# Converting the weights to bf16 once, in device memory, and giving the weight loads and the small transfers different DMA queues

## The chip, the cores and the metric

The kernel runs on all 8 cores of one Trainium2 chip. Every core does the same work on its own part of the batch. The metric is device time in microseconds (us) of the slowest core, and lower is better. Cores 0 to 3 are one die of the chip, cores 4 to 7 the other.

Names in the profiles: PE is TensorE (matmuls) and PEld its weight loads, DVE is VectorE, ACT ScalarE, POOL GpSimd and SP SyncE. HBM is the device memory, SBUF the memory on the core, and a DMA moves data between or within them. The granted clock is the share of its full clock at which PE was allowed to run.

- An execution on 8 cores can fall into a slower state, in which one die or both run matmuls at a lower granted clock: in one execution of e1 a core of die 0 took 40042 us at 0.719 and a core of die 1 40826 us at 0.701.
- The experiments ran on two chips that are called the second and the third here; the first comparison is taken as another, the first chip (the record names no chip for it). In the experiments the clock was often lower: the kernel before took 38.8 ms in the first comparison (clock 0.703 to 0.705 in the profiled run) and in fast executions 39.5 to 39.7 ms there (0.674 to 0.695). Whole times of different chips are therefore never compared. Inside a trace, the short stages that the argument needs are compared, and most of those are bound by DMA (share 0.93 to 1.08 in the conversions and the sample FFNs before) or by waits, not by the clock.
- Ratios compare fast runs with fast runs. The medians quoted with the experiments are of all runs, slow ones too, so a ratio is not quite that of the medians.

## The reference, cut to what matters

It is a four-layer encoder. The FFN weights are 1024 x 4096 and 4096 x 1024, and all weights arrive as float32.

```python
def encoder_layer(x, prm, ...):
    x = x + 0.5 * swiglu_ffn(rms_norm(x, ffn1_norm), ffn1_w_gate, ffn1_w_up, ffn1_w_down)
    proj = rms_norm(x, mix_norm) @ w_in
    # S5 state space, differential attention, conv module, gMLP: the "mixer"
    x = x + concat(a_out, b_out, c_out, d_out) @ w_out
    x = x + memory_cross_attention(rms_norm(x, xattn_norm), mem_k, mem_v, xattn_wq, xattn_wo)
    x = x + 0.5 * swiglu_ffn(rms_norm(x, ffn2_norm), ffn2_w_gate, ffn2_w_up, ffn2_w_down)
# ... the small inputs, the outputs and the second request group are cut
```

A core handles 4096 prompt tokens and 256 sample tokens. Both use the same weights.

## The kernel before

The kernel has its own small scheduler. It keeps one instruction list for each engine, and derives each wait from the last writer and the readers of a buffer. The tokens are taken in nine tiles: eight prompt tiles of 512 tokens and one sample tile of 256. Each tile goes through all four layers, so every weight is loaded nine times.

Weights go through a ring of four SBUF slots of 1 MB (128 x 4096 bf16). The loads are issued on GpSimd's queue (`pool`). They read float32 from HBM and write bf16 into SBUF, so the DMA itself converts: the page below has 2270.65 MB on that queue, where bytes are counted as written, and 4716.93 MB read from HBM in all.

```python
NRING = 4
def w_issue_upto(n):                       # ...
        tag, src, shp = wq_list[i]         # src: a float32 view of the weight in HBM
        slot = ring[i % NRING]
        # ...
        P.DMA("pool", dst, src)

def w_next(tag):
    i = wstate["taken"]
    w_issue_upto(i + NRING - 1)            # at step i, the loads up to i+2 are issued
    # ...
```

One FFN takes 24 ring slots and 768 matmuls of 512 columns:

```python
def ffn(l, which, N, gidx):
    A.reset()                              # a barrier, see below
    rmsnorm_to_h(N, gains_sb[:, l, gidx, :])
    # ...
    for half in range(2):
        for jc in range(4):
            wg = w_next(which + "g")
            wu = w_next(which + "u")
            # 4 x (8 + 8) matmuls, one silu and one product each
        for oc in range(4):
            wd = w_next(which + "d")
            # 2 x 16 matmuls, one residual add each
```

Every stage (FFN, mixer, cross-attention) opens with `A.reset()`, which puts a barrier into all five instruction lists. A barrier waits for all engines and for every DMA that had been issued by then in program order:

```python
def barrier(self, with_dma=True):
    for e in COMPUTE + ("sp",):
        # ... e waits for the instruction counts of the other engines, and
        for key, cnt in self.dma_cnt.items():
            if self.waited[e].get(key, 0) < 16 * cnt:
                waits[key] = 16 * cnt
```

The main loop is `prep()` (tables, and the keys and values of the memory), then for each tile and each layer `ffn("ffn1")`, `mixer`, `xattn`, `ffn("ffn2")`. Small inputs, outputs and saved keys and values go over SyncE's queue (`sp`), apart from the small ones that are converted on the way, such as `wsT`, which share GpSimd's queue with the ring.

The softmax here doesn't subtract the row's maximum and nothing guards it: scores larger than these inputs give would overflow.

## Time and profile before

The median of the 20 runs is 38774 us (38658 to 38866). The profiled run's slowest core is core 1.

| what | before |
|---|---|
| span of core 1 | 38652.5 us |
| start and preparation | 435 us |
| eight prompt tiles | 3754 us (first) to 4795 us (last) |
| sample tile | 3823 us |
| one FFN, prompt tile / sample tile | about 200 / 172 us |

Stage times in this document run from the first matmul of a stage's normalisation to the first of the next stage's, in one core's trace. The last normalisation of a tile counts to the next tile.

First some lines of the page of the kernel before: busy time of the engines; DMA share in 40 slices; queues as packets, MB and share of 16 engines; the chain of work that ended last; and the ring's loads with count, size and median time from issue to landing.

```profile
span 38652.5 us, 393341 instructions; the slowest of 8 cores (38538.2 to 38652.5 us)
...
PE 22710.2 (59%) x127946; PEld 11272.6 (29%) x127946; DVE 11651.9 (30%) x20752; ACT 7756.2 (20%) x15712; POOL 3130.1 (8%) x3366
...
DMA  3444444444444433434444433344432344325665
...
q0 software_dynamic: 2898592, 2270.65, 42.2%
q1 hardware_dynamic: 92896, 260.74, 1.9%
...
HBM read 4716.93 MB, written 84.78 MB: 124 GB/s over the span
...
PE 48%; DVE 21%; DMA 15%; issue 8%; ACT 5%; POOL 2%; DVEq 1%; ACTq 0%; POOLq 0%; SPq 0%
...
ring<-ffn_w_gate POOLq DMA_DIRECT2D x576, 1024.0 KB, 12.2
ring<-ffn_w_up POOLq DMA_DIRECT2D x576, 1024.0 KB, 15.2
ring<-ffn_w_down POOLq DMA_DIRECT2D x576, 1024.0 KB, 13.0
```

No engine is full. The chain runs through PE for half the time. That DMA is 15% of the chain and busy 42% overall says nothing yet about where a faster load would help. The stretch view does. Its columns are the stretch and its length, busy us of PE, PE weight load, DVE, ACT and POOL, the granted clock, the DMA share (the times of all packets added up, so that a full stretch can come out slightly above 1, as the 1.07 below) and GB/s written. The first line is a prompt FFN, the second two sample FFNs, on core 1.

```profile
10220.00:10408.00 188.00, 171.25 (x768) 75.69 (x768) 33.09 (x48) 25.18 (x41) 22.25 (x23) 0.96 0.92 126
35640.00:35970.00 330.00, 203.79 (x1543) 162.66 (x1540) 46.19 (x105) 32.15 (x76) 44.48 (x46) 0.82 1.07 148
```

In the prompt tile the DMA engines are almost full, but PE is busy 171 of 188 us: the loads just keep up. In the sample tile each matmul has half the columns, the loads are the same size, and DMA is the limit (share 1.07, PE busy 204 of 330 us). The timeline of PE in that prompt FFN shows how small the waits are. Columns: start, length, what, and in brackets the idle time before it and what ended it.

```profile
10220.05 32.20 PE L201 MATMUL PS<-h,ring 128*128 128x512 bf16 x136 [12.44 <-DVE h L245]
10252.66 13.97 PE L201 MATMUL PS<-h,ring 128*128 128x512 bf16 x64 [0.42 <-DMA ring<-ffn_w_up]
10269.50 13.93 PE L201 MATMUL PS<-h,ring 128*128 128x512 bf16 x56 [2.86 <-DMA ring<-ffn_w_up]
```

A last pair of lines is from the waits view of core 1: total us, times, longest. The second is for `wsT`, the gMLP weight that stands behind ring loads in GpSimd's queue.

```profile
PE PS L201 <- DMA ring<-ffn_w_up: 540.4, 243, 8.7
...
DVE arena L222 <- DMA arena<-wsT: 383.2, 36, 13.8
```

### The profile page before, as it was taken

To read this page: it belongs to the slowest core of one execution; us is meant where nothing else is said; L and a number is where in the kernel's file an instruction comes from. 1 tells how busy PE (TensorE), PEld (TensorE's weight loads), DVE (VectorE), ACT (ScalarE), POOL (GpSimd) and SP (SyncE) were. 2 spreads that over 40 slices of the span, in tenths; PEclk is the share of its full clock that TensorE was granted. 3 is DMA by queue.
4 is the path that set the end of the run, shared out by engine and by line. 5 is a ranking of instruction groups with operands and counts; after the bars stand their busy time and mean duration, and the time that the engine had idled before them with its cause. 6 is when DMAs were issued, how large, how long until landed. Compare 5 with 4: busy or idle time off the path is not lost.

```text
span 38652.5 us, 393341 instructions; the slowest of 8 cores (38538.2 to 38652.5 us)
## 1 busy us (share of the span) xinstructions
PE 22710.2 (59%) x127946; PEld 11272.6 (29%) x127946; DVE 11651.9 (30%) x20752; ACT 7756.2 (20%) x15712; POOL 3130.1 (8%) x3366
## 2 busy tenths in 40 slices
PE   3555555556666655556656655666765666764444
PEld 1222222222222222223223322332333323333333
DVE  3333333333333333332332233223223232222222
ACT  0111111111111112122112222221222212221111
POOL 0000000000000000000000000000000000001111
PEclk8777777777777766767777766677766677666666
DMA  3444444444444433434444433344432344325665
GB/s 70 69 69 69 74 69 69 69 74 70 70 70 70 65 57 58 62 56 65 71 71 74 59 49 53 61 72 72 67 50 48 57 72 72 56 43 80 82 81 79
DMA packets 2993473, 2556.56 MB, mean 66 GB/s; under 512 B 187135, under 2 KB 2905983, under 8 KB 2984192
## 3 DMA queue, kind: packets, MB, share of 16 engines
q0 software_dynamic: 2898592, 2270.65, 42.2%
q1 hardware_dynamic: 92896, 260.74, 1.9%
q8 instruction: 1088, 17.83, 0.2%
q14 instruction: 897, 7.35, 0.1%
HBM read 4716.93 MB, written 84.78 MB: 124 GB/s over the span
## 4 chain that ended last, share of the span: by engine, by line
PE 48%; DVE 21%; DMA 15%; issue 8%; ACT 5%; POOL 2%; DVEq 1%; ACTq 0%; POOLq 0%; SPq 0%
PE PS L201 48%; DMA ring<-ffn_w_up 8%; DVE arena L254 5%; DVE arena L222 5%; ACT arena L219 4%; DVE arena L265 4%; DVE h L245 2%; DVE arena L235 2%; POOL arena L222 2%; DMA arena<-wsT 1%; DMA arena<-cv 1%; ACT L219 1%; DMA arena<-Bx 1%; DVEq L165 1%; DVE arena L245 1%
## 5 line engine op out<-in xcount | busy, mean ns | idle before, releaser
L201 PE MATMUL PS<-h,ring 128*128 128x512 bf16 (+1 forms) x41472 | 9018.2, 381 | 2292.1 <-DVE h L245 1677.3
L201 PEld LDWEIGHTS PS<-h,ring 128*128 128x128 bf16 x41472 | 4167.0, 101 | 7179.5 <-issue 3023.9
L201 PE MATMUL PS<-arena 128*128 128x64 bf16 (+4 forms) x12354 | 1282.7, 265 | 6696.2 <-POOL arena L222 4082.5
L219 ACT ACTIVATE arena<-PS 128x512 f32<-128x512 f32 (+7 forms) x4298 | 2247.2, 524 | 11509.8 <-PE PS L201 10354.7
L201 PE MATMUL PS<-arena,ring 128*128 128x512 bf16 (+1 forms) x19712 | 4192.1, 375 | 449.9 <-DVE arena L222 285.9
L219 ACT ACTIVATE arena<-PS,alibi 128x256 bf16<-128x256 f32 (+1 forms) x8960 | 3677.0, 458 | 1548.1 <-PE PS L201 1538.3
L222 DVE TENSOR_TENSOR arena<-arena,PS 128x512 bf16<-128x512 f32 (+2 forms) x2376 | 1564.6, 659 | 7685.0 <-PE PS L201 7022.0
L201 PEld LDWEIGHTS PS<-arena 128*128 128x128 bf16 (+2 forms) x12354 | 782.6, 132 | 7168.5 <-issue 7130.9
L201 PE MATMUL PS<-arena,VAh 128*65 128x128 bf16 x16896 | 2725.0, 312 | 227.1 <-ACT arena L219 227.1
L201 PEld LDWEIGHTS PS<-arena,ring 128*128 128x128 bf16 x19712 | 1944.4, 100 | 2710.4 <-issue 723.8
L201 PE MATMUL PS<-QT,KTh 32*128 32x128 bf16 x16896 | 2347.9, 275 | 547.5 <-ACT arena L219 289.6
L219 ACT ACT_TABLE_LOAD x513 | 658.2, 1283 | 8944.3 <-DVE arena L245 5753.2
L222 DVE TENSOR_TENSOR PS<-PS,diag 128x128 f32<-128x128 f32 (+1 forms) x1152 | 307.6, 289 | 5862.1 <-PE PS L201 5799.4
L201 PEld LDWEIGHTS PS<-arena,VAh 128*65 128x65 bf16 x16896 | 1678.5, 160 | 795.4 <-issue 331.0
L254 DVE RECIPROCAL arena<-PS 64x512 f32<-64x512 f32 (+3 forms) x480 | 1379.0, 2873 | 1371.7 <-PE PS L201 1371.7
L254 DVE RECIPROCAL arena<-arena 128x512 f32<-128x512 f32 (+5 forms) x374 | 1065.3, 2848 | 2408.0 <-ACT arena L219 2324.0
L245 DVE SCALAR_TENSOR_TENSOR x<-PS,x 128x512 f32<-128x512 f32 (+1 forms) x1152 | 762.9, 662 | 3292.1 <-PE PS L201 3292.1
L201 PE MATMUL PS<-arena,ones_b 128*128 128x512 bf16 (+2 forms) x1616 | 700.5, 571 | 1689.9 <-ACT arena L219 1689.9
L265 DVE TENSOR_TENSOR_SCAN arena<-arena,sst 128x64 f32<-128x64 f32 x4096 | 1437.7, 351 | 451.5 <-DVE arena L222 40.2
L201 PEld LDWEIGHTS PS<-QT,KTh 32*128 32x128 bf16 x16896 | 1004.8, 99 | 1884.1 <-issue 1633.9
L219 ACT ACTIVATE arena<-x 128x512 bf16<-128x512 f32 (+1 forms) x1224 | 741.1, 605 | 3966.6 <-issue 2107.5
L222 DVE TENSOR_TENSOR arena<-PS,arena 128x512 f32<-128x512 f32 (+2 forms) x1316 | 803.3, 662 | 2095.8 <-PE PS L201 2074.9
(110 smaller groups left out, 12910.1 us busy)
## 6 DMA issues: line engine op xcount, KB each, us to landing
ring<-ffn_w_gate POOLq DMA_DIRECT2D x576, 1024.0 KB, 12.2
ring<-ffn_w_up POOLq DMA_DIRECT2D x576, 1024.0 KB, 15.2
ring<-ffn_w_down POOLq DMA_DIRECT2D x576, 1024.0 KB, 13.0
ring<-w_in POOLq DMA_DIRECT2D x144, 1024.0 KB, 10.9
arena<-s5tab SPq DMA_DIRECT2D x36, 2560.0 KB, 10.6
ring<-w_out POOLq DMA_DIRECT2D x72, 1024.0 KB, 12.4
arena<-Cx POOLq DMA_DIRECT2D x72, 512.0 KB, 6.2
ring<-xattn_wq POOLq DMA_DIRECT2D x36, 1024.0 KB, 9.3
```

What stands on the lines that cost most here:

```text
L165: e.wait_ge(sems[k], v)
L201: self.S.op("pe", lambda e: e.matmul(o.ap, lhsT=l.ap, rhs=r.ap, start=start, stop=stop, **kw), reads=[l.buf, r.buf], writes=[o.buf])
L219: self.S.op("act", lambda e: e.activation(out=o.ap, in_=i.ap, func=func, **kw), reads=reads, writes=[o.buf])
L222: self.S.op(eng, lambda e: e.tensor_tensor(out=o.ap, in0=a.ap, in1=b.ap, op=op), reads=[a.buf, b.buf], writes=[o.buf])
L235: self.S.op(eng, lambda e: e.tensor_scalar(out=o.ap, in0=a.ap, scalar1=v1, scalar2=None, op0=op0), reads=reads, writes=[o.buf])
L245: self.S.op(eng, lambda e: e.scalar_tensor_tensor(out=o.ap, in0=a.ap, scalar=v, in1=b.ap, op0=op0, op1=op1), reads=reads, writes=[o.buf])
L254: self.S.op("dve", lambda e: e.reciprocal(out=o.ap, in_=i.ap), reads=[i.buf], writes=[o.buf])
L265: self.S.op("dve", lambda e: e.tensor_tensor_scan(out=o.ap, data0=d0.ap, data1=d1.ap, initial=iv, op0=ALU.mult, op1=ALU.add), reads=reads, ...
```

## The change

Intent: read each float32 weight once instead of nine times. A DMA from HBM to HBM converts it into a bf16 copy; the nine ring loads then read half the bytes. A ring load no longer converts and is issued on SyncE's queue, and the small transfers move to GpSimd's. The core of the diff:

```diff
+    def convert_weights(l_, only=None):
+        order = ["ffn1_w_gate", "ffn1_w_up", "ffn1_w_down", "w_in", "w_out", "xattn_wq", "xattn_wo",
+                 "ffn2_w_gate", "ffn2_w_up", "ffn2_w_down"]
...
+                half = rows // 2
+                P.DMA("pool", dst[0:half], src[0:half], grp="cv")
+                P.DMA("pool", dst[half:rows], src[half:rows], grp="cv")
...
-            P.DMA("pool", dst, src)                     # the ring load
+            P.DMA("sp", dst, src)
...
-                wq_list.append((which + "g", kview(g, l, 0, D, c0, 512), (8, 512)))
+                wq_list.append((which + "g", bview(g, l, 0, D, c0, 512), (8, 512)))   # bf16 copy; all weights alike
...
-        P.DMA("sp", dst, src)                           # every small DMA alike
+        P.DMA("pool", dst, src)
...
     def main_program():
+        for l_ in range(L):
+            convert_weights(l_, only=["xattn_wk", "xattn_wv"])
+        convert_weights(0)
         prep()
...
             for l in range(L):
+                if (kind, ti) == tiles[0] and l + 1 < L:
+                    convert_weights(l + 1)
                 ffn(l, "ffn1", N, 0)
```

The two halves of a weight write the same scheduler buffer, so the second half waits until the first has landed. Each core makes its own copies.

Why the queues move along with it: the author left every DMA that converts on GpSimd's queue and gave SyncE the ring loads once they had nothing to convert. In the trace before, all ring loads are issued on GpSimd's queue (576 of each of the three FFN weights); in the trace after, the same numbers on SyncE's, and all of them are bf16 to bf16. No run here tries a cast on another queue.

More of the change, by code (lines that the diff above doesn't have):

```diff
@@ L106, in op, with dma @@
         self._mark(tok, reads, writes)
-    def dma(self, q, fn, reads=(), writes=()):
-        j = self.dma_rr[q]
-        self.dma_rr[q] = (j + 1) % NDMA_SEMS
-        key = "dma_%s_%d" % (q, j)
+    def dma(self, q, fn, reads=(), writes=(), grp=None, ngrp=6):
+        if grp is None:
+            j = self.dma_rr[q]
+            self.dma_rr[q] = (j + 1) % NDMA_SEMS
+            key = "dma_%s_%d" % (q, j)
+        else:
+            j = self.dma_rr.get(grp, 0)
+            self.dma_rr[grp] = (j + 1) % ngrp
+            key = "dma_%s_%d" % (grp, j)
         prev = self.dma_cnt.get(key, 0)
@@ L266, in SCAN, with DMA @@
                   reads=reads, writes=[o.buf])
-    def DMA(self, q, o, i):
+    def DMA(self, q, o, i, grp=None):
         if len(o.ap.shape) > 3 and len(i.ap.shape) == len(o.ap.shape):
@@ L276, in DMA @@
                 pass
-        self.S.dma(q, lambda e: e.dma_start(out=o.ap, in_=i.ap), reads=[i.buf], writes=[o.buf])
+        self.S.dma(q, lambda e: e.dma_start(out=o.ap, in_=i.ap), reads=[i.buf], writes=[o.buf], grp=grp)
 def build(TP=TP_FULL, L=L_FULL):
@@ L410, in build @@
     A = Arena()
+    WB = {}
+    for nm_ in ["ffn1_w_gate", "ffn1_w_up", "ffn1_w_down", "ffn2_w_gate", "ffn2_w_up", "ffn2_w_down", "w_in", "w_out",
+                "xattn_wq", "xattn_wk", "xattn_wv", "xattn_wo"]:
+        shp_ = list(Wn[nm_].ap.shape)
+        tb_ = nc.dram_tensor(nm_ + "_b16", shp_, BF16, kind="Internal").ap()
+        WB[nm_] = [T(tb_[l_], Buf("%s_b16_%d" % (nm_, l_))) for l_ in range(L)]
+    def convert_weights(l_, only=None):
+        order = ["ffn1_w_gate", "ffn1_w_up", "ffn1_w_down", "w_in", "w_out", "xattn_wq", "xattn_wo",
+                 "ffn2_w_gate", "ffn2_w_up", "ffn2_w_down"]
+        if only is not None:
+            order = only
+        if True:
+            for nm_ in order:
+                src = T(Wn[nm_].ap[l_], Wn[nm_].buf)
+                dst = WB[nm_][l_]
+                rows, cols = src.ap.shape
+                if cols > 2048:
+                    src = src.re("r (a b) -> r a b", b=2048)
+                    dst = dst.re("r (a b) -> r a b", b=2048)
+                half = rows // 2
+                P.DMA("pool", dst[0:half], src[0:half], grp="cv")
+                P.DMA("pool", dst[half:rows], src[half:rows], grp="cv")
     wq_list = []
@@ L444, in kview, with bview @@
         return T(w.ap[l, r0:r0 + nr, c0:c0 + ncol].rearrange("(k p) n -> p k n", p=128), w.buf)
+    def bview(nm, l, r0, nr, c0, ncol):
+        wb = WB[nm][l]
+        return T(wb.ap[r0:r0 + nr, c0:c0 + ncol].rearrange("(k p) n -> p k n", p=128), wb.buf)
     def plan_ffn(l, which):
-        g, u, d = Wn[which + "_w_gate"], Wn[which + "_w_up"], Wn[which + "_w_down"]
+        g, u, d = which + "_w_gate", which + "_w_up", which + "_w_down"
         for half in range(2):
@@ L450, in plan_ffn @@
                 c0 = 2048 * half + 512 * jc
-                wq_list.append((which + "g", kview(g, l, 0, D, c0, 512), (8, 512)))
-                wq_list.append((which + "u", kview(u, l, 0, D, c0, 512), (8, 512)))
+                wq_list.append((which + "g", bview(g, l, 0, D, c0, 512), (8, 512)))
+                wq_list.append((which + "u", bview(u, l, 0, D, c0, 512), (8, 512)))
             for oc in range(4):
-                wq_list.append((which + "d", kview(d, l, 2048 * half, 2048, 256 * oc, 256), (16, 256)))
+                wq_list.append((which + "d", bview(d, l, 2048 * half, 2048, 256 * oc, 256), (16, 256)))
     def plan_layer(l):
@@ L458, in plan_layer @@
         for c in range(4):
-            wq_list.append(("win", kview(Wn["w_in"], l, 0, D, 512 * c, 512), (8, 512)))
+            wq_list.append(("win", bview("w_in", l, 0, D, 512 * c, 512), (8, 512)))
         for c in range(2):
-            wq_list.append(("wout", kview(Wn["w_out"], l, 0, D, 512 * c, 512), (8, 512)))
-        wq_list.append(("wq", kview(Wn["xattn_wq"], l, 0, D, 0, 512), (8, 512)))
-        wq_list.append(("wo", kview(Wn["xattn_wo"], l, 0, 512, 0, D), (4, 1024)))
+            wq_list.append(("wout", bview("w_out", l, 0, D, 512 * c, 512), (8, 512)))
+        wq_list.append(("wq", bview("xattn_wq", l, 0, D, 0, 512), (8, 512)))
+        wq_list.append(("wo", bview("xattn_wo", l, 0, 512, 0, D), (4, 1024)))
         plan_ffn(l, "ffn2")
     for l in range(L):
-        wq_list.append(("wk", kview(Wn["xattn_wk"], l, 0, D, 0, 512), (8, 512)))
-        wq_list.append(("wv", kview(Wn["xattn_wv"], l, 0, D, 0, 512), (8, 512)))
+        wq_list.append(("wk", bview("xattn_wk", l, 0, D, 0, 512), (8, 512)))
+        wq_list.append(("wv", bview("xattn_wv", l, 0, D, 0, 512), (8, 512)))
     tiles = [("p", i) for i in range(NT)] + [("s", 0)]
@@ L534, in prep @@
         sc = A.alloc(L * 3 * 16, name="sc").re("p (l a g) -> p l a g", l=L, a=3)
-        P.DMA("sp", sc, ssm_sc)
+        P.DMA("pool", sc, ssm_sc)
         lq = A.alloc(L * 4 * 32, parts=1, name="lq").re("p (l a d) -> p l a d", l=L, a=4)
-        P.DMA("sp", lq, lqk)
+        P.DMA("pool", lq, lqk)
         pr = A.alloc(L * 2 * 32, parts=1, name="pr").re("p (l a d) -> p l a d", l=L, a=2)
@@ L617, in prep @@
             P.TS(Etab[:, l, 1, :], SN[:, :, 63], sgn)
-            P.DMA("sp", T(s5tab.ap[l], s5tab.buf), TB.re("p a g j -> p (a g j)"))
+            P.DMA("pool", T(s5tab.ap[l], s5tab.buf), TB.re("p a g j -> p (a g j)"))
             A.off -= (16 * 15 + 11 * 1024)
@@ L622, in prep @@
         memf = A.alloc(8 * 256, name="memf").re("p (k n) -> p k n", k=8)
-        P.DMA("sp", memf, T(memT.ap.rearrange("(k p) n -> p k n", p=128), memT.buf))
+        P.DMA("pool", memf, T(memT.ap.rearrange("(k p) n -> p k n", p=128), memT.buf))
         sq = A.alloc(8 * 256, BF16, name="msq").re("p (k n) -> p k n", k=8)
@@ L645, in prep @@
                 P.ACT(st_, o, AF.Copy)
-                P.DMA("sp", T(o_mkT.ap[l, 128 * m:128 * m + 128, :], o_mkT.buf), st_)
+                P.DMA("pool", T(o_mkT.ap[l, 128 * m:128 * m + 128, :], o_mkT.buf), st_)
             for c in range(2):
@@ L652, in prep @@
                 P.ACT(st_, o, AF.Copy)
-                P.DMA("sp", T(o_mv.ap[l, 128 * c:128 * c + 128, :], o_mv.buf), st_)
+                P.DMA("pool", T(o_mv.ap[l, 128 * c:128 * c + 128, :], o_mv.buf), st_)
     def sincos(dst, phi, tmp, tmi, tmk, shift):
@@ L678, in mixer @@
         if kind == "p" and ti > 0:
-            P.DMA("sp", KTh[:, :, 0:t0], T(kth_d.ap[l, :, :, 0:t0], kth_d.buf))
-            P.DMA("sp", VAh[:, 0:4 * ti].re("p j h d -> p j (h d)"), T(vah_d.ap[l, :, 0:4 * ti, :], vah_d.buf))
+            P.DMA("pool", KTh[:, :, 0:t0], T(kth_d.ap[l, :, :, 0:t0], kth_d.buf))
+            P.DMA("pool", VAh[:, 0:4 * ti].re("p j h d -> p j (h d)"), T(vah_d.ap[l, :, 0:4 * ti, :], vah_d.buf))
         zsig = A.alloc(2 * 512, name="zsig").re("p (k n) -> p k n", k=2)
@@ L700, in mixer @@
                 P.CP(KTh[:, m, t0:t0 + N], kstage[:, m, 0:N], eng="pool")
-                P.DMA("sp", T(o_kT_p.ap[l, 128 * m:128 * m + 128, t0:t0 + N], o_kT_p.buf), kstage[:, m, 0:N])
+                P.DMA("pool", T(o_kT_p.ap[l, 128 * m:128 * m + 128, t0:t0 + N], o_kT_p.buf), kstage[:, m, 0:N])
             else:
                 P.CP(KTown[:, m, :], kstage[:, m, 0:N], eng="pool")
-                P.DMA("sp", T(o_kT_s.ap[l, 128 * m:128 * m + 128, :], o_kT_s.buf), kstage[:, m, 0:N])
+                P.DMA("pool", T(o_kT_s.ap[l, 128 * m:128 * m + 128, :], o_kT_s.buf), kstage[:, m, 0:N])
         if kind == "p":
@@ L711, in mixer @@
                 P.CP(VAh[:, 4 * ti + c, :, 0:64], vstage[:, c, :].re("p (h d) -> p h d", h=4), eng="pool")
-            P.DMA("sp", T(o_v_p.ap[l, t0:t0 + 512, :].rearrange("(c p) n -> p c n", p=128), o_v_p.buf), vstage)
+            P.DMA("pool", T(o_v_p.ap[l, t0:t0 + 512, :].rearrange("(c p) n -> p c n", p=128), o_v_p.buf), vstage)
             if ti < NT - 1:
-                P.DMA("sp", T(kth_d.ap[l, :, :, t0:t0 + 512], kth_d.buf), KTh[:, :, t0:t0 + 512])
-                P.DMA("sp", T(vah_d.ap[l, :, 4 * ti:4 * ti + 4, :], vah_d.buf), VAh[:, 4 * ti:4 * ti + 4].re("p j h d -> p j (h d)"))
+                P.DMA("pool", T(kth_d.ap[l, :, :, t0:t0 + 512], kth_d.buf), KTh[:, :, t0:t0 + 512])
+                P.DMA("pool", T(vah_d.ap[l, :, 4 * ti:4 * ti + 4, :], vah_d.buf), VAh[:, 4 * ti:4 * ti + 4].re("p j h d -> p j (h d)"))
         else:
@@ L722, in mixer @@
                 P.CP(VAown[:, s_, :, 0:64], vstage[0:64, s_, :].re("p (h d) -> p h d", h=4), eng="pool")
-            P.DMA("sp", T(o_v_s.ap[l].rearrange("(s p) n -> p s n", p=64), o_v_s.buf), vstage[0:64])
+            P.DMA("pool", T(o_v_s.ap[l].rearrange("(s p) n -> p s n", p=64), o_v_s.buf), vstage[0:64])
         phase_done()
@@ L776, in mixer @@
         if kind == "s":
-            P.DMA("sp", T(o_gv_s.ap[l].rearrange("(c p) n -> p c n", p=128), o_gv_s.buf), gvt[:, 0:nch, :])
+            P.DMA("pool", T(o_gv_s.ap[l].rearrange("(c p) n -> p c n", p=128), o_gv_s.buf), gvt[:, 0:nch, :])
         tmpm = A.alloc(128, name="tmpm")
@@ L800, in mixer @@
                 for m in range(2):
-                    P.DMA("sp", T(o_conv_p.ap[l, 128 * m:128 * m + 128, :], o_conv_p.buf), zsig[:, m, 482:512])
+                    P.DMA("pool", T(o_conv_p.ap[l, 128 * m:128 * m + 128, :], o_conv_p.buf), zsig[:, m, 482:512])
         else:
@@ L804, in mixer @@
             cbf = A.alloc(2 * NSS * 30, name="cbf").re("p (k s n) -> p k s n", k=2, s=NSS)
-            P.DMA("sp", cbf, T(cbuf.ap[:, l], cbuf.buf))
+            P.DMA("pool", cbf, T(cbuf.ap[:, l], cbuf.buf))
             for m in range(2):
@@ L808, in mixer @@
                 P.CP(zv4[:, m, :, 30:94], zsig[:, m, 0:NS].re("p (s n) -> p s n", s=NSS))
-                P.DMA("sp", T(o_conv_s.ap[l, :, 128 * m:128 * m + 128, :].rearrange("s p n -> p s n"), o_conv_s.buf),
+                P.DMA("pool", T(o_conv_s.ap[l, :, 128 * m:128 * m + 128, :].rearrange("s p n -> p s n"), o_conv_s.buf),
                       zsig[:, m, 0:NS].re("p (s n) -> p s n", s=NSS)[:, :, 34:64])
@@ L852, in build @@
     gm_sb = P.sb("gm_sb", [128, L, 2, 256])
-    P.DMA("sp", gm_sb, gm_gb)
+    P.DMA("pool", gm_sb, gm_gb)
     def ln_feature_major(v, N, gT, bT):
@@ L879, in s5 @@
         TB = A.alloc(5 * 1024, name="TBl").re("p (a g j) -> p a g j", a=5, g=16)
-        P.DMA("sp", TB.re("p a g j -> p (a g j)"), T(s5tab.ap[l], s5tab.buf))
+        P.DMA("pool", TB.re("p a g j -> p (a g j)"), T(s5tab.ap[l], s5tab.buf))
         Bw = A.alloc(2 * 16 * 128, BF16, name="Bw").re("p (a g n) -> p a g n", a=2, g=16)
@@ L898, in s5 @@
             s0sb = A.alloc(NSS * 16, name="s0sb").re("p (s g) -> p s g", s=NSS)
-            P.DMA("sp", s0sb, T(s0.ap[:, l], s0.buf))
+            P.DMA("pool", s0sb, T(s0.ap[:, l], s0.buf))
             send = A.alloc(NSS * 16, name="send").re("p (s g) -> p s g", s=NSS)
@@ L944, in s5 @@
             if ti == NT - 1:
-                P.DMA("sp", T(o_ssm_p.ap[l], o_ssm_p.buf), sst[l])
+                P.DMA("pool", T(o_ssm_p.ap[l], o_ssm_p.buf), sst[l])
         else:
-            P.DMA("sp", T(o_ssm_s.ap[l].rearrange("s p g -> p s g"), o_ssm_s.buf), send)
+            P.DMA("pool", T(o_ssm_s.ap[l].rearrange("s p g -> p s g"), o_ssm_s.buf), send)
         S.barrier()
@@ L1111, in main_program @@
             if kind == "p":
-                P.DMA("sp", x, T(xT_p.ap[:, 512 * ti:512 * ti + 512].rearrange("(k p) n -> p k n", p=128), xT_p.buf))
+                P.DMA("pool", x, T(xT_p.ap[:, 512 * ti:512 * ti + 512].rearrange("(k p) n -> p k n", p=128), xT_p.buf))
             else:
-                P.DMA("sp", x[:, :, 0:N], T(xT_s.ap.rearrange("(k p) n -> p k n", p=128), xT_s.buf))
+                P.DMA("pool", x[:, :, 0:N], T(xT_s.ap.rearrange("(k p) n -> p k n", p=128), xT_s.buf))
             for l in range(L):
+                if (kind, ti) == tiles[0] and l + 1 < L:
+                    convert_weights(l + 1)
                 ffn(l, "ffn1", N, 0)
@@ L1137, in main_program @@
             if kind == "p":
-                P.DMA("sp", T(yT_p.ap[:, 512 * ti:512 * ti + 512].rearrange("(k p) n -> p k n", p=128), yT_p.buf), yo)
+                P.DMA("pool", T(yT_p.ap[:, 512 * ti:512 * ti + 512].rearrange("(k p) n -> p k n", p=128), yT_p.buf), yo)
             else:
-                P.DMA("sp", T(yT_s.ap.rearrange("(k p) n -> p k n", p=128), yT_s.buf), yo[:, :, 0:N])
+                P.DMA("pool", T(yT_s.ap.rearrange("(k p) n -> p k n", p=128), yT_s.buf), yo[:, :, 0:N])
         assert wstate["taken"] == len(wq_list), (wstate, len(wq_list))
```

## The prediction

> **What bounds the kernel now.** The page gives PE 59% busy of 38652 us, DMA 44%. No engine is full: the chain that ended last is PE 48%, DVE 21%, DMA 15%. Phases end in barriers on all engines and DMAs.
>
> fp32 weight loads cost little in eight of nine token tiles. In a prompt FFN (10220 to 10408 us, stretch table) PE is busy 171 of 188 us; a gate/up pair of loads takes about 18 us to land, against 14 us of matmuls, DMA share 1.0. In the prompt part (to 34845 us) the waits view gives PE 330 us of waiting for ring loads. In the sample tile (34845 to 38652 us) matmuls are half as long, loads the same: two FFNs (35640 to 35970) take 330 us, PE busy 204, DMA share 1.07 at 148 GB/s written. There PE waits 376 us for ring loads, ACT at barriers about 370 more (xattn_wo 185, w_up 97, w_in 87, nearly all here).
>
> **Savings (estimates from those durations).**
> - Prompt ring waits: 300 us.
> - Sample tile: bf16 halves the bytes read; FFN pairs should fall to about 210 us, barrier waits shrink: 550 us.
> - The mixer's wsT load queues behind two w_out loads (15.5 us to landing; DVE waits 11 us). With weights on SP it should land in time: 5 us x 36, about 200 us.
> - Memory K/V preparation: 50 us.
> - Against it: s5tab now stands ahead of Bx in one queue, and o_kT_p stores leave later: minus 130 us.
> Together about 970 us; ceiling near 1400 us.
>
> [...]
>
> **Cost.** Each core converts 121.6 M weights: 487 MB read, 243 MB written. Layer l+1's conversion is issued before layer l's first FFN, whose opening barrier waits for every DMA semaphore, the conversion's too (the changed kernel's instruction order shows SP's first weight load behind them). So nothing hides it: four stalls, one before the preparation. [...] This trace's most saturated stretch reads 2 x 148 = 296 GB/s, into SBUF; a copy that also writes HBM should read 180 to 240 GB/s: 2.0 to 2.7 ms. I take 2.35 ms.
>
> **Net:** 38765 + 2350 - 970 = about 40150 us, 3.6% slower; range 39350 to 41300. Chances: faster 0.03, within 2% 0.15, slower 0.82.
>
> **What would show it.**
> - Four stretches (start, and ahead of layers 0 to 2 of the first tile), each 500 to 700 us, PE idle, DMA full.
> - Prompt tiles from the second on: each only 40 to 60 us of 4.3 ms faster.
> - Sample tile: 3807 us down to about 3250.
> - Ring loads landing in 6 to 9 us instead of 12 to 15; PE's waits for them nearly gone in prompt tiles.
> - DVE's 383 us of waiting for wsT gone.
> - HBM read down from 4717 MB by about 1.6 GB.
>
> **What would make it wrong.** [...] casts between HBM addresses at half the assumed rate (then near 42500); part of it overlapping with work; loads in 512 B and 1 KB rows no faster (no sample gain); freed GpSimd order helping more phases than wsT.

## The result, and the profile after

| | before | after |
|---|---|---|
| median us | 38774 (20 runs) | 39718 (10 runs) |
| lowest to highest | 38658 to 38866 | 39581 to 39922 |

The ratio of the fast runs is 1.0244 (95% interval 1.0227 to 1.026): the changed kernel is slower by 2.4%. Its outputs are correct. The prediction was 40150 us in a range of 39350 to 41300, with 0.82 on slower.

The page of the changed kernel (its slowest core is core 7):

```profile
span 39771.0 us, 393483 instructions; the slowest of 8 cores (39543.7 to 39771.0 us)
...
DMA  6664422222222222222222211122222111222434
...
q1 hardware_dynamic: 2676352, 2122.45, 18.1%
q0 software_dynamic: 274496, 652.22, 9.5%
...
HBM read 3081.15 MB, written 328.05 MB: 86 GB/s over the span
...
PE 54%; DVE 20%; issue 7%; DMA 6%; ACT 5%; another core or an unknown queue 3%; POOL 2%; DVEq 1%; SPq 0%; ACTq 0%; POOLq 0%
...
ring<-ffn_w_gate_b SPq DMA_DIRECT2D x576, 1024.0 KB, 5.5
ring<-ffn_w_up_b SPq DMA_DIRECT2D x576, 1024.0 KB, 7.5
ring<-ffn_w_down_b SPq DMA_DIRECT2D x576, 1024.0 KB, 7.3
```

HBM reads fell by 4716.93 - 3081.15 = 1636 MB, ring loads land in half the time, and DMA was halved over most of the span. All of that was the aim, and the kernel is slower. The DMA row shows where: its first three digits are 6 instead of 3 and 4.

The stage table says how much. Both columns are core 1, with a mean granted clock of 0.705 in both traces.

| stage (us) | before | after | difference |
|---|---|---|---|
| start to the preparation's normalisation | 301.1 | 912.3 | +611 |
| from there to the first FFN | 133.9 | 648.9 | +515 |
| tile 0, layer 0, second FFN | 199.1 | 619.2 | +420 |
| tile 0, layer 1, second FFN | 197.6 | 620.0 | +422 |
| tile 0, all the rest | 3357.7 | 3303.0 | -55 |
| tiles 1 to 7, FFNs | 11558.9 | 11147.2 | -412 |
| tiles 1 to 7, mixers | 16982.6 | 16851.9 | -131 |
| tiles 1 to 7, cross-attention | 2098.9 | 2097.8 | -1 |
| sample tile | 3822.8 | 3343.4 | -479 |
| whole span | 38652.5 | 39543.7 | +891 |

The four stages that grew add up to 1969 us, and everything else saved 1078 us. The savings are real: over the four cores of die 0 the prompt FFNs of tiles 1 to 7 fell by 241 to 412 us and the mixers by 104 to 175 us. The cost is larger. (The medians differ by 944 us, 53 more than core 1: the slowest core of the run after is core 7, at a granted clock of 0.700, and some of its prompt FFNs took 221 to 227 us at 0.79 to 0.82.)

The stretch view of core 7 for three of the four stages that grew:

```profile
94.00:629.00 535.00, 0.00 (x0) 0.00 (x0) 0.00 (x0) 0.00 (x0) 9.84 (x20) 1.00 0.93 111
1024.00:1560.00 536.00, 0.00 (x0) 0.00 (x0) 0.00 (x0) 0.00 (x0) 10.09 (x20) 0.50 0.93 113
2314.00:2912.00 598.00, 180.70 (x712) 74.21 (x712) 39.66 (x53) 27.30 (x43) 10.14 (x20) 0.64 0.98 135
```

The first two are as predicted: a conversion with DMA nearly full and PE with not one instruction. The third is not. While 20 conversion DMAs run, PE does 712 matmuls. The conversions of layers 2 and 3 did overlap with work, which the prediction left out of its sum.

The waits view of core 7 (the first two lines are the waits that held the start and the first FFN), with a rate to work out: a layer without the memory weights has 29.4 M weights, 117.4 MB read and 58.7 MB written, in 536 us: 219 GB/s read, 329 GB/s read and written.

```profile
DVE arena L227 <- DMA arena<-lqk: 629.6, 1, 629.6
...
ACT arena L224 <- DMA ffn_w_down_b<-ffn_w_down: 543.2, 1, 543.2
...
PE PS L206 <- DMA ring<-ffn_w_up_b: 368.7, 44, 75.5
...
DVE arena L227 <- DMA arena<-wsT: 58.9, 27, 7.8
```

And in the sample tile, two FFNs on core 1 after the change, in the same columns as before:

```profile
36950.00:37170.00 220.00, 178.73 (x1545) 153.21 (x1544) 51.82 (x114) 35.41 (x82) 0.00 (x0) 0.91 0.78 224
```

330 us became 220 us, and DMA is no longer full.

### Why the third conversion overlapped

GpSimd's timeline in the changed kernel, core 7, around the end of layer 0:

```profile
2241.09 0.71 POOL L282 DMA_DIRECT2D arena<-o_mv  x1 [1.47 <-issue]
2314.61 0.55 POOL L282 DMA_DIRECT2D ffn_w_gate_b<-ffn_w_gate  x1 [72.81 <-DVE x L227]
2362.07 0.54 POOL L282 DMA_DIRECT2D ffn_w_gate_b<-ffn_w_gate  x1 [46.91 <-DMA ffn_w_gate_b<-ffn_w_gate]
2362.60 0.52 POOL L282 DMA_DIRECT2D ffn_w_up_b<-ffn_w_up  x1
```

In program order the conversion of layer 2 comes after the second FFN of layer 0. But the change took the ring loads off GpSimd, and with them the last thing that GpSimd had to do in an FFN. Past that FFN's opening barrier (DVE's residual add, at 2314) the next entry in its list is the conversion. So it issues it while PE is at the start of the FFN, not at the end. PE's timeline in the same stretch:

```profile
2335.93 17.16 PE L206 MATMUL PS<-h,ring 128*128 128x512 bf16 x72 [12.41 <-DVE h L250]
2364.29 16.60 PE L206 MATMUL PS<-h,ring 128*128 128x512 bf16 x64 [11.20 <-DMA ring<-ffn_w_up_b]
2447.33 16.05 PE L206 MATMUL PS<-h,ring 128*128 128x512 bf16 x64 [66.44 <-DMA ring<-ffn_w_up_b]
```

The DMA view of core 7 for 2314 to 2912 us says how long an up-projection's ring load took here from issue to landing (the last number, a median):

```profile
ring<-ffn_w_up_b SPq DMA_DIRECT2D x7, 1024.0 KB, 53.6
```

Over the whole run it is 7.5 us. The two kinds of transfer differ in the size of their packets: in the 535 us of a conversion alone the DMA view (core 7) counts 2145 packets for 59.25 MB, 27.6 KB each, or about 32.7 KB without the 336 that are under 512 B, while a stretch of plain ring loads has 12421 packets for 8.45 MB, 0.68 KB each. The author's guess was that the long waits come from the large packets; this trace does not show it. Experiment e9 tests the idea.

### The profile page after: what moved, and what is told of

Its sections match the earlier page's. It is cut to its first block, busy times and chain, and to the rows that moved or that the text cites. A ratio compares the mean times of both kernels' runs of the same rounds, so it can differ in the third digit from the quotient of the medians.

```text
span 39771.0 us, 393483 instructions; the slowest of 8 cores (39543.7 to 39771.0 us)
## 1 busy us (share of the span) xinstructions
PE 22734.1 (57%) x127946; PEld 11277.9 (28%) x127946; DVE 11654.2 (29%) x20752; ACT 7758.7 (20%) x15712; POOL 1479.0 (4%) x1793
## 3 DMA queue, kind: packets, MB, share of 16 engines
HBM read 3081.15 MB, written 328.05 MB: 86 GB/s over the span
## 4 chain that ended last, share of the span: by engine, by line
PE 54%; DVE 20%; issue 7%; DMA 6%; ACT 5%; another core or an unknown queue 3%; POOL 2%; DVEq 1%; SPq 0%; ACTq 0%; POOLq 0%
PE PS L206 54%; DVE arena L259 5%; DVE arena L227 5%; ACT arena L224 4%; DVE arena L270 4%; DVE h L250 2%; DVE arena L240 2%; POOL arena L227 2%; DMA arena<-Bx 1%; ACT L224 1%; DMA arena<-cv 1%; DMA ring<-ffn_w_up_b 1%; DVEq L170 1%; DVE mix L227 1%
```

## The experiments

The theory (T) after the result: the cost is the volume of the conversion at a fixed rate, and two of four conversions were partly hidden because GpSimd ran ahead; the savings come from the halved bytes. The main rivals:

- R1: the chain of halves inside a conversion, one waiting for the other, costs the time, not the volume.
- R2: the savings come from the queue (SyncE against GpSimd), not from the bytes.
- R3: reading the copy back some other way, or making it without a separate pass, would cost as much.

Ten experiments ran: e1 to e4 on the second chip in one series, e6 to e9 on it in another, e5 and e10 on the third chip; e10 is the kernel of e7 again. The kernel before ran in each series.

### e1: all conversions ahead of the preparation

```diff
-        convert_weights(0)
+        for l_ in range(L):
+            convert_weights(l_)
...
-                if (kind, ti) == tiles[0] and l + 1 < L:
-                    convert_weights(l + 1)
```

> The changed kernel, but all four layers are converted before the preparation, so that no conversion can overlap matmuls. My theory: in the changed kernel the conversions of layers 2 and 3 (counted from 0) ran ahead into the FFN of the layer before, each stretching it by about 420 us (199 to 620) where a conversion alone takes 536 us; undone, that costs 2 x 115: about 39950 us (39900 to 40000), a start of about 2240 us without a matmul, and every second FFN of the first tile back at 195 us. Rival: the DMA engines were full in the overlap too (share 0.98), so nothing was hidden and the time stays at 39720 us.

Measured: correct, median 40755 us, ratio to before 1.0259 (1.0161 to 1.0356), formally unclear at 2%. On core 1 the start took 2540.0 us, which is 2239 more than before (301.1); the stage after it was back at 123.2 us, and the second FFNs of layers 0 and 1 at 194.6 and 193.9 us. One stretch line shows it, with 80 DMA issues on GpSimd and nothing on any other engine:

```profile
94.00:2200.00 2106.00, 0.00 (x0) 0.00 (x0) 0.00 (x0) 0.00 (x0) 39.96 (x80) 1.00 0.94 109
```

What follows: without overlap the conversion costs 2239 us. In the changed kernel the same conversions cost 611 us at the start and, by e2 below, 1381 us later, 1992 in all. So the overlap hid about 250 us, near the 230 that was expected. (The 1969 of the table is lower by what the other work in those stages saved.) The forecast of the whole time can't be judged on another chip.

### e2: convert one layer only (wrong result)

```diff
-        wb = WB[nm][l]
+        wb = WB[nm][0 if nm not in ("xattn_wk", "xattn_wv") else l]
...
-                if (kind, ti) == tiles[0] and l + 1 < L:
-                    convert_weights(l + 1)
```

Every layer reads the copies of layer 0, so the outputs are wrong; the work is otherwise the same.

> The changed kernel, but only layer 0 is converted and all layers read its copies (results wrong on purpose beyond the first layer; loads, matmuls and queues as in the changed kernel). My theory: three conversions cost 515 + 420 + 422 us, so about 38360 us (38280 to 38450), 1.1% faster than before the change. Rival: the slowdown comes from the new queue order (small transfers behind each other on GpSimd's queue, spread over all tiles) and the conversion is mostly harmless: 39300 us or more.

Measured: median 39568 us beside 39682 for the kernel before, but four of the five runs were slow. The one fast run took 38832 us, beside 39643 us in the mean of the two fast ones of the kernel before: faster, and between the two forecasts. The stages decide. On core 1 the start stayed at 920.2, the next stage was 117.8 instead of 648.9, the two second FFNs 195.3 and 193.7 instead of 619.2 and 620.0. The three conversions are thus worth 531 + 424 + 426 = 1381 us, and the other rows of the stage table stayed within about 1% of the changed kernel's (the sample tile: 3379 us against 3343). Cost and savings are separate things.

### e3: bf16 copies, but the queues as before

The cut shows the edit against the changed kernel.

```diff
-            P.DMA("sp", dst, src)          # ring load
+            P.DMA("pool", dst, src)
...
-        P.DMA("pool", dst, src)            # every small DMA alike
+        P.DMA("sp", dst, src)
```

> The conversion alone without the change of queues: bf16 weights are loaded by GpSimd's queue, all other transfers stay on SP as before. My theory (the gain is in the bytes, the queue only sets order): ring loads still land in 6 to 9 us, the sample tile takes 3350 to 3420 us, but GpSimd now has ring loads to issue in every FFN and cannot run ahead to the next conversion, so all four conversions stand alone (+230 us), and wsT again waits behind w_out loads (+60 to 150 us): 40000 to 40120 us. Rival: the gain comes from issuing weights on SP rather than GpSimd: ring loads land in 12 us or more, the sample tile is back at 3800 us, over 40500 us in all.

Measured: correct, 40623 us, ratio 1.0224 (1.0094 to 1.0354), unclear. Two lines of its page:

```profile
q0 software_dynamic: 781728, 2513.93, 24.9%
...
ring<-ffn_w_up_b POOLq DMA_DIRECT2D x576, 1024.0 KB, 8.1
```

By its page, the gate, up and down loads land in 6.1, 8.1 and 8.6 us, almost as on SyncE (5.5, 7.5, 7.3). The sample tile took 3357 us (3343 with the split), and the mixers of tiles 1 to 7 took 16835 us, no more than the 16852 with the split: the loss that was expected from `wsT` did not come. R2 is rejected: the savings are the bytes. The change of issuing engine moved these three landing times by at most 1.3 us.

Two further readings. First, the start took 910.7 us although the small loads of the preparation were on SyncE again, not behind the conversions in GpSimd's queue. The `lqk` wait above looked like a queue that is blocked, but the opening barrier alone is enough to hold the preparation. Second, GpSimd's timeline (core 7) shows the conversion of layer 2 now at the end of the FFN, behind the last ring load:

```profile
2445.27 0.88 POOL L282 DMA_DIRECT2D ring<-ffn_w_up_b  x1 [6.02 <-PE PS L206]
2446.14 0.56 POOL L282 DMA_DIRECT2D ffn_w_gate_b<-ffn_w_gate  x1
```

The two second FFNs grew to 718.8 and 719.1 us: 195 us of FFN and then 524 us of conversion. The queue split did save time, 200 us for the two stages together, but by letting GpSimd run ahead.

### e4: no conversion pass, tile 0 writes its ring slots back

Tile 0 loads float32 on GpSimd as before and stores each filled slot as a 128 x 4096 bf16 block. Later tiles load the block, whose rows are 8 KB long, on SyncE, and from then on small transfers go over GpSimd's queue (not in the cut).

```diff
-            P.DMA("pool", dst, src)
+            if i < 2 * L + NIT:                          # preparation and tile 0
+                P.DMA("pool", dst, src)
+            else:
+                P.DMA("sp", slot, WBT[(i - 2 * L) % NIT])
...
+        if 2 * L <= i < 2 * L + NIT:                     # in w_next
+            P.DMA("sp", WBT[i - 2 * L], ring[i % NRING], grp="wb")   # barriers skip this group
```

> A version meant to beat both: in the first tile the weights are loaded in fp32 as before, and each loaded bf16 tile is stored from SBUF to memory by SP (1 MB each, 235 MB in all, nothing read again; the stores are left out of the barriers); later tiles load these copies on SP in rows of 8 KB, small transfers then go to GpSimd's queue as in the changed kernel. My theory: the conversion's 1970 us shrink to under 100 us, the savings of tiles 1 to 8 (about 1030 us) stay: 37750 us (37600 to 37950). Rival: the stores crowd out the fp32 loads, which already fill the DMA engines in each FFN of the first tile; the first tile grows by 500 us or more: over 38200 us.

Measured: correct, 39139 us, ratio 0.9851 (0.9789 to 0.9912): faster, though not surely by 2%. The start and preparation stages are as before the change (299.8 and 129.1 us). Tile 0 took 4293 us, about 540 more than before: the DMA engines, already at 0.9 in a prompt FFN, now carry a store for each load (share 1.03 to 1.04), and the FFNs stretch from about 199 us to between 255 and 262. (Some 14 us of each are the lower clock of that chip: PE was busy about 185 us at 0.85 to 0.88 granted, instead of 172 at 0.94.) The sample tile took 3314 us. The copy costs 540 us this way instead of 1969, so R3 is rejected. Two things differ: the float32 read is one that tile 0 has to do anyway, and the stores run beside matmuls; no run weighs the one against the other. But the theory's "under 100 us" was wrong and its rival right: tile 0 has no room for the stores. That leads to e7.

### e6: up to six conversions in flight at once

This is e1 with the second half of each weight on its own scheduler buffer, so no conversion waits for its other half.

```diff
-                P.DMA("pool", dst[half:rows], src[half:rows], grp="cv")
+                P.DMA("pool", T(dst.ap[half:rows], WB2[nm_][l_].buf), src[half:rows], grp="cv")
```

> The run with all conversions first (e1_conv_first), but the second half of a weight no longer waits for its first half, so up to six copies are in flight instead of two. The time of the start until the first normalisation's matmuls was 2540 us there (core 1), 2239 more than before the change. My theory: the copies are limited by what the DMA engines and the memory move (about 330 GB/s read and written together), so the start stays within 3% of 2540 us. Rival: the waits between halves cost the 7% that the DMA share of 0.93 leaves: the start falls by 140 us or more.

Measured (one look, correct, the profile fell in the slow state; PE has not one instruction from 94 to 2200 us, so its clock does not enter there): 2539.2 us to the preparation's normalisation, against 2540.0 in e1. R1 is rejected: the chain of halves costs nothing. A conversion DMA of 4 MB (a half of a gate weight) took 95.9 us instead of 42.3 from issue to landing with more of them in flight; the sum was the same. The stretch line of e6 beside that of e1 (above) shows it:

```profile
94.00:2200.00 2106.00, 0.00 (x0) 0.00 (x0) 0.00 (x0) 0.00 (x0) 38.11 (x75) 1.00 1.00 109
```

The DMA share rose from 0.94 to 1.00 and the rate stayed at 109 GB/s written. So the idle share of the engines was not what held the conversion back. What sets the rate, the DMA engines or the memory behind them, no run separates.

### e9: conversion in small pieces

The columns are converted in blocks of 512, so that a conversion row is 1 KB of bf16. Each block has its own buffer, so these DMAs are also no longer chained in halves.

```diff
-                half = rows // 2
-                P.DMA("pool", dst[0:half], src[0:half], grp="cv")
-                P.DMA("pool", dst[half:rows], src[half:rows], grp="cv")
+                for c_ in range(0, cols, 512):           # weights of 512 columns stay as they were
+                    P.DMA("pool", T(dst.ap[:, c_:c_ + 512], Buf()), src[:, c_:c_ + 512], grp="cv")
```

> The changed kernel, but each copy of the conversion moves column blocks of 512 elements, so that it runs in pieces of 2 KB read and 1 KB written, as the weight loads do, instead of 64 KB and 32 KB. My theory: in the second FFN of layers 0 and 1 of the first tile, which a conversion overlaps, the large pieces starve the weight loads (PE waits 66 to 75 us for one pair); [...] no wait of PE for a ring load over 30 us there. The stage still ends with the conversion, so it stays at 580 to 700 us. A conversion alone takes 536 us or more (to 650). Rival: the DMA engines are simply full, the size of the pieces does not matter: PE still waits 60 us or more for single loads.

Measured (one look, correct): packets in the conversion's first 535 us rose from 2145 to 54856 (core 7, 56.95 MB, 4% less, so 1.04 KB each), and the conversion alone was about as long as before (926 and 652 us for the two opening stages on core 1, against 912 and 649). In the overlapped FFN the long waits are gone. PE's timeline on core 1:

```profile
2368.53 14.97 PE L206 MATMUL PS<-h,ring 128*128 128x512 bf16 x56 [10.54 <-DMA ring<-ffn_w_up_b]
2383.81 1.89 PE L206 MATMUL PS<-h,ring 128*128 128x512 bf16 x8 [0.30 <-DMA ring<-ffn_w_gate_b]
2401.96 13.63 PE L206 MATMUL PS<-h,ring 128*128 128x512 bf16 x56 [16.27 <-DMA ring<-ffn_w_up_b]
```

The longest wait for a ring load fell from 72.2 to 17.0 us. That fits the guess about large packets and does not prove it. (The edit also removed the chain; e6 shows that the chain does not set the conversion's rate, but e6 had no FFN beside it, so for the waits the two are not separated.) And yet the stage was 612.3 us, against 619.2. The edit changed how the waiting was spread; it did not shorten the stage, because the two jobs together fill the DMA engines (share 1.02 from 2314 to 2912 us on core 1). An estimate from the traces: 536 us of conversion alone plus 24 ring loads of 1 MB at the roughly 330 GB/s that the DMA view shows while plain bf16 loads run (about 3.2 us each, 76 us) is 612 us. Against 195 + 536 us one after the other, the overlap can save about 120 us a stage.

### e5: the kernel before, with wsT on the other queue

```diff
-        wsr = A.alloc(512, BF16, name="wsr")...
-            P.DMA("pool", wsr, T(wsT.ap[l], wsT.buf))
+        wsr = A.alloc(512, name="wsr")...
+            P.DMA("sp", wsr, T(wsT.ap[l], wsT.buf))     # float32, read so by DVE
```

> The kernel before, with one load moved: wsT comes in fp32 on SP's queue instead of as a cast behind two w_out loads on GpSimd's. Read from the stages, since the granted clock of this chip moves by a few per cent. My theory: this is the part of the mixer's saving that comes from order and not from bytes: DVE's 383 us of waiting for wsT falls under 80 us and the mixer stages of the prompt tiles get 3 to 5 us shorter each. Rival: w_out or other loads take the time back: the mixer stages stay within 1 us of those before.

Measured (one look, correct; one fast run of 39691 us beside a mean of 39585 us in four fast ones of the kernel before; the profile fell in the slow state, so only the undisturbed die 0 is read): compared with the first chip's trace, DVE's wait for `wsT` (in the mixers of all nine tiles) fell from 441 to 142 us on core 0 and from 383 to 168 us on core 1, not under 80. The 28 mixers of tiles 1 to 7 fell by 135 us on core 0 and 58 us on core 1, and over the four cores by 58 to 171 us, 2 to 6 us each, where 3 to 5 had been expected. The changed kernel's mixers fell by 104 to 175 us on these cores, so moving this one load brings much the same gain. The wait can be taken away, but only a part of it lay on the critical path: 216 to 287 us of wait less on cores 1 and 2, 58 and 171 us of mixers. In the whole time no gain shows.

### e7: spread the write-back over the eight prompt tiles

Load j of a tile's 224 is stored back in tile j modulo 8, and read as bf16 from then on. The stores go over SyncE and are left out of the barriers, as in e4; queues and small transfers otherwise stay as before.

```diff
-            P.DMA("pool", dst, src)
+            t_, j_ = wb_place(i)                         # tile, place in the tile
+            if t_ > j_ % 8:
+                P.DMA("pool", slot, WBT[j_])
+            else:
+                P.DMA("pool", dst, src)
...
+        if t_ == j_ % 8:                                 # in w_next
+            P.DMA("sp", WBT[j_], ring[i % NRING], grp="wb")
```

> The kernel before, with SBUF copies stored as in e4_writeback, but spread: prompt tile t stores only each eighth weight tile (28 of 224, residue t), and a weight tile is loaded as a bf16 copy from the tile after its store on. All weight loads stay on GpSimd's queue, small transfers and stores on SP. My theory: the stores cost 540 us in e4_writeback only because the first tile's DMA engines were full; spread, each new store is paid by loads that have become light: first tile +60 to 130 us, prompt tiles from the third on 50 to 90 us faster each than before, sample tile 3300 to 3380 us: 850 us less than the kernel before of the same rounds (700 to 1000), ratio 0.978. Rival: a store costs the same 2.4 us wherever it is placed: 490 us less, ratio 0.987.

Measured: correct, median 38830 us beside 39686, ratio 0.9763 (0.9693 to 0.9834). It is surely faster than the kernel before, but not surely by 2%, so the formal verdict is unclear; the rival's 0.987 lies outside the interval. On core 2 the start and preparation are untouched (301.5 and 136.3 us). Tile 0 took 3947 us, 191 more than the same core of the first trace, where 60 to 130 had been expected. Part of that is the clock: among the FFNs of tile 0 one of 211 us had 0.92 granted and PE busy 175 us, one of 230 us had 0.78 and PE busy 208 us. The sample tile took 3250 us, 579 less than core 2 of the first trace (3829). Its two FFNs in a stretch line:

```profile
35690.00:35890.00 200.00, 175.67 (x1538) 152.38 (x1539) 46.21 (x105) 32.14 (x76) 24.29 (x46) 0.94 0.68 242
```

200 us for what took 330 before and 220 in the changed kernel.

### e8: e7, with the ring loads left out of the barriers

```diff
-                    if key.startswith("dma_wb"):
+                    if key.startswith(("dma_wb", "dma_rg")):
...
-                P.DMA("pool", slot, WBT[j_])
+                P.DMA("pool", slot, WBT[j_], grp="rg")
```

> As e7_spread, and the barriers no longer wait for weight loads (the ring is not in the arena that the barriers protect; each load is still ordered by its own semaphores). My theory: the barriers' waits for prefetched weights (before the change about 370 us on ACT, nearly all in the sample tile) are part of what bf16 copies shorten already, so little is left: 50 to 200 us less than e7_spread, mainly in the sample tile. Rival: freed prefetches collide with the loads that a phase needs first (wsT, Bx), and the gain is nil.

Measured: correct, median 38870 us, ratio 0.9723 (0.9632 to 0.9813), unclear at 2%; the profile fell in the slow state. Against e7 the sample tile is 10 us shorter (3241 us) and nothing else stands out. In the sample tile of e7 ACT already waits for no ring load at a barrier (257 us before the change), so nothing is left to free there. In its prompt tiles ACT still waited 175 us for them (core 2), in e8 not at all, and yet no gain stands out. The edit isn't worth its risk.

### e10: e7 again, on another chip

> e7_spread once more, for a narrower interval. My theory: the gain is one of bytes and does not depend on the chip's clock: ratio 0.976 (0.970 to 0.983) to the kernel before, sample tile 3200 to 3300 us. Rival: the 0.976 of the first time was luck of the clock: 0.985 or more.

Measured: correct, median 39050 us (6 runs) beside 39493 (11 runs) of the kernel before. Most executions there were slow. Two fast ones of e10 (mean 38875) stand against four of the kernel before (mean 39585): 0.982 by that, too few for an interval. The sample tile is again short (3250 us on core 5, 3305 on core 1). It confirms the direction, and not a size; 0.982 lies at the upper edge of the theory's range.

## Why the prediction was right, and where it was off

**The direction and the mechanism were right.** It said that float32 loads cost little in eight of nine tiles, so that halving their bytes saves about 1 ms, and that the conversion costs more than that. Measured on core 1: 1078 us saved, 1969 us spent, 891 us net (970, 2350 and 1380 predicted). The predicted time was 432 us too high, inside the range: the cost was put too high and the savings too low, and the two errors add up. One step of the mechanism failed, the overlap.

**The conversion: 2350 predicted, 1969 measured.** Two steps of that term differ.

- "So nothing hides it: four stalls" failed for two of the four. The opening barrier does hold SyncE and PE, but GpSimd issues the conversion as soon as its own list allows. The prediction checked the order on SyncE and not on GpSimd, whose list has nothing between the opening barrier of the second FFN and the next conversion. e1 puts the overlap at about 250 us, and e3, where GpSimd is kept busy until the FFN's end, at 200 us. The prediction did name "part of it overlapping with work" among the things that would make it wrong.
- The rate was assumed a little low. Four stalls without overlap cost 2239 us (e1), not 2350. A conversion alone reads and writes 329 GB/s, 219 of them read. The prediction's bracket, 180 to 240 GB/s read, which the author estimated beside the 296 GB/s read in the trace's two sample FFNs, holds the measured 219.

**The savings: 970 predicted, 1078 measured.** The sum was closer than its terms, and that is luck: a loss of 130 us that never came and a prompt term that was 112 us larger made up for three terms that were 39 to 71 us smaller.

- Prompt ring waits, 300 predicted. The FFNs of tiles 1 to 7 fell by 412 us on core 1, 241 to 412 over die 0; about 7 us an FFN at most, to 194 us, with matmuls back to back. PE's waits for the ring between 6000 and 34800 us had been 289 us on core 1, and there are none left after. Over these 56 FFNs on core 1, PE's idle time fell by 300 us, as predicted, and its busy time by 123 us, at a mean granted clock of 0.935 before and 0.941 after. Why PE was busy for less time, beyond that bit of clock, was not found.
- Sample tile, 550 predicted: 479 measured. The prediction's 210 us for two FFNs was measured as 220. Its barrier waits of 370 us were not "nearly all here": 257 us lay in the sample tile and 112 us, of `xattn_wo`, in the prompt part.
- `wsT`, 200 predicted: the wait fell from 383 to 59 us on core 1, but the mixers of tiles 1 to 7 fell by 131 us only. e5 gains about as much over die 0 by moving this load alone, and in e3 the wait is still 241 us with the mixers just as short. So the saving is there, by the order or by the bytes, but the wait's length is not its size, and its cause is not fully settled.
- Memory keys and values, 50 predicted: 11 measured (133.9 to 123.2 us in e1, where no conversion stands in that stage).
- Order of the small transfers, minus 130 predicted: no stage shows it. The mixers got shorter, not longer.

**The signs it named.** Prompt tiles "40 to 60 us" faster were in fact 57 to 90 us faster on core 1. The sample tile went to 3343 us, not 3250. Ring loads at 6 to 9 us land in 5.5 to 7.5. PE's ring waits in the prompt part are gone, the `wsT` wait nearly so, and HBM reads fell by 1636 MB as said. Of "four stretches, PE idle, DMA full" two were there, at 535 and 536 us, and two were not.

**What beats both kernels.** The idea was good and its place was bad. Storing the slot that a tile has loaded and converted anyway adds only the store (224 of 1 MB, each 7.5 us from issue to landing in e7). Over eight tiles (e7) it costs nothing at the start and 191 us in tile 0 of core 2, part of which is the clock; and it is faster than the kernel before on the same chip (0.976), where the changed kernel was slower on its own (1.024). The two were not run side by side.

## What to carry to other kernels

Before paying for a conversion pass, count in which stages the loads it speeds up are really waited for; here nearly half of the saving (479 of 1078 us on core 1) came from one tile in nine, and the pass read every weight once more, two layers of four in stretches in which PE had not one instruction (535 and 536 us). If the data passes through on-chip memory anyway, write it back from there, in small portions over stages that have DMA time to spare. And to tell what will overlap, read each engine's own instruction list between two barriers: moving work off an engine lets it run ahead to whatever stands next in its list, as GpSimd did here (about 200 us against e3).

## What the runs measured of the hardware

- A copy from HBM to HBM that casts, with all 8 cores at it: a core read 219 GB/s of float32 and wrote 110 GB/s of bf16, and neither more DMAs in flight (2539.2 against 2540.0 us) nor smaller rows (56.95 against 59.25 MB written in 535 us) changed that by more than 4%.
- Ring loads beside such copies, whose packets were of 27.6 KB: a 1 MB load of small packets (0.68 KB) that lands in 7.5 us over the whole run kept PE waiting up to 75.5 us (core 7; 72.2 us on core 1); with conversion packets of about 1 KB, and no chain of halves, the longest wait was 17.0 us (core 1).
- The granted clock of a prompt FFN, all 8 cores running the same program: after the change most had 0.93 to 0.95 granted (192 to 196 us on core 1). Others had less within one execution: 0.79 to 0.82 on core 7 of the first comparison (221 to 227 us), and 0.78 (229 to 231 us) beside 0.94 (195 us) on core 1 of e3. What decides between the two is not shown.
